# Half of a_u by seven block products, its bias prepared off VectorE, the softmax factor on ScalarE

## The chip, the cores and the metric

One Trainium2 chip, one core. The time is the device time of one execution of the whole program, in microseconds (us); the median of several executions is given. Engines are called PE (TensorE matmuls), PEld (its weight loads), DVE (VectorE), ACT (ScalarE), POOL (GpSimd) and SP (the sequencer that issues most loads).

## The reference, cut to what matters

One decoder block on 512 tokens with 1024 channels. The parts that the change touches:

```python
z = h @ w_in                        # columns: a_u | a_v | q | k | v | qi | ki | wi | g_a | g_b
y_a = gelu(a_u) * mixed             # a_u: 512 x 1024
# mixed, for chunk n of 128 tokens and group g of 128 channels:
#   sum_s tril(w_s[g])[t, s] * layer_norm(gelu(a_v))[n, s, g, c] + b_s[g, t]
p = softmax(att)                    # attention: 4 blocks of 128 queries, 8 heads, selected keys
o = p @ v
merged = sigmoid(g_a) * (y_a @ w_proj_a) + sigmoid(g_b) * (y_b @ w_proj_b)
mod = silu(c) @ w_ada + b_ada       # six sections of 1024: shift, scale, gate, twice
```

layer_norm has a gain ln_g and an offset ln_b for each channel. So mixed is the product of the masked w_s with the normalized values, times ln_g, plus a bias `ln_b * rowsum(tril(w_s)) + b_s`, and it is this bias that the kernel prepares.

## The kernel before, in words

Every fp32 product is three fp32r products: each operand is split into a high part `hi` (a copy, ACT, line 134) and a rest `lo` (a subtraction, DVE or POOL, line 138). Weights come as chunks of 128 x 1024 floats into three raw buffers; `get(i, ahead)` issues loads ahead and emits `hi` and `lo` of the chunk `ahead` places further on (`ensure`, `prep`). All engines run their instructions in the order in which the program emits them; that order is written out by hand, as lists of small tasks for each step.

The stages around the change, in order: a_v (lines 923 to 946, steps `vs` 0 to 7), which also holds the index scores; a_u (line 1051), four groups of two chunks, each chunk 24 matmuls of 512 columns; then twice `xround` (lines 1095 to 1136), which makes half of g_a by seven block products instead of eight, followed each time by two groups of the projection of y_a (`W_PA`). A round is 7 x 8 x 3 = 168 matmuls of 256 columns. Its seven weight chunks are blocks of w_in or sums of blocks, and the sums are made in DRAM by POOL's transfers (`x_moves`, line 265, eight for a round, one of them at each call of `x_move`).

`au_tasks` and `au_post` run before and after each chunk of these stages, with the step numbers of `austep`. They hold the normalization of a_v, `mix_mm` and `mix_ev` (the mixing, eight times), `rs_mm` and `bias_mix` (the row sums by a product with ones, and the bias, eight DVE instructions), and the top-k selection (`BG`: 35 pieces). The modulation's dot products (`dot`, line 209, 128 x 1024 on DVE, each behind a load of 512 KB) are put between weight chunks in the stream: eight beside a_u, four beside `W_PA`, eight beside `W_GB`, four beside `W_PB`.

The attention loop (lines 1260 to 1281) has 16 units: the query blocks i = 3, 2, 1, 0 in that order, four pairs of heads each; block i has (i + 1) x 128 keys. At step s it emits, in this order: the product with v of unit s - 3 (`at_pv`) and its split `yh` (ACT), `yl` (DVE); scores and maximum of unit s (`at_qk` on PE, `at_soft_a` on DVE); transposes of unit s - 2 (`at_T`) with the split `th` (ACT), `tl` (DVE); the softmax factor of unit s - 1 (`at_soft_b`, DVE: a reciprocal and two multiplications); the split `qh` (ACT), `ql` (DVE) of the queries of unit s + 2; the exponential of unit s (`at_exp`, ACT); and `gb_part`, a share of the product for g_b (`W_GB`), which in steps 1, 2, 6, 8, 10, 12, 14 and 16 also emits `hi` and `lo` of one weight chunk, and with it, where there is one, a dot product ahead of them. `at_pv` of unit s - 3 reads the `tl` of the step before.

Of the kernel before, what the change touches and what calls it, by code (L numbers as in the profile page):

```python
# [16 lines left out]
S = 512  # L17
# [11 lines left out]
def block_kernel(ctx: ExitStack, tc: tile.TileContext, x, x_t, c_row, positions, w_ada_t, w_first, w_in, w_blocks,  # L29
                 gmlp_w_s, gmlp_b_s, w_proj_a, w_proj_b,  # L30
                 w_out, w_ffn_in, w_ffn_out, final_norm_g, small, consts, out):
# [226 lines left out]
    W_AV = [[add_w(w_in, [k0, k0 + 1], 1024 + 512 * h, 512, V if k0 % 4 else P) for k0 in range(0, 8, 2)] for h in range(2)]  # L258
    W_AU = [group(w_in, 256 * g, pool=2, mods=mm_, mraw="acc") for g in range(4)]
    xsum = {(r, n): dram.tile([128, 1024], F32, name=f"xsum{r}{n}") for r in range(2) for n in (1, 2, 3, 4)}  # L260

# [8 lines left out]

    xm = [fn for r in range(2) for fn in x_moves(r)]

# [616 lines left out]

    def load_bs():  # L890
        late["bsb"] = mid.tile([128, 8, 128], F32, name="bsb", tag="A3", bufs=1)
        P.dma_start(late["bsb"], bass.AP(tensor=gmlp_b_s.tensor, offset=gmlp_b_s.offset,
                                         ap=[[0, 128], [128, 8], [1, 128]]))

# [4 lines left out]
    def mask_ws():  # L899
        P.affine_select(late["wmT"], late["wmT"], pattern=[[0, 8], [1, 128]], compare_op=OP.is_ge, fill=0.0, base=0,  # L900
                        channel_multiplier=-1)
        late["ones"] = mid.tile([128, 2, 128], F32, name="ones2", tag="ql", bufs=2)[:, 0]
        P.memset(late["ones"], 1.0)

    VT = {0: [load_ws, lambda: rows_a(1), lambda: rows_b(1)],
          1: [lambda: h_hi("S1"), lambda: h_hi("S4"), lambda: h_lo("S1"), lambda: h_lo("S4")],
          2: [lambda: rows_a(2), lambda: rows_b(2), lambda: h_hi("S3")],
          3: [lambda: h_lo("S3")],
          5: [mask_ws],
          7: [load_bs]}  # L910
    for _ in range(16):
# [12 lines left out]
    for h in range(2):  # L924
        pb = [bank(k, "pav") for k in range(4)]
        for i in W_AV[h]:
            for fn in VT.get(vs, []):
                fn()
            if vs % 2:
                x_move()  # L930
            if iu[1] < 24:
                idx_accs()
            else:
                run_bg(2.0)
            if vs in (5, 6):
# [46 lines left out]

    def rs_mm():
        late["rs"] = [bank(5 + k, "rs") for k in range(2)]
        for k, p in enumerate(late["rs"]):
            T.matmul(p, late["ones"], late["wmT"][:, 4 * k:4 * k + 4].rearrange("p a n -> p (a n)"), start=True, stop=True)

    def bias_mix():
        for m in range(8):
            b = late["bsb"][:, m]  # L990
            V.scalar_tensor_tensor(b, late["rs"][m // 4][:, 128 * (m % 4):128 * (m % 4) + 128], lnbc[:, m:m + 1], b,
                                   op0=OP.mult, op1=OP.add)

    ub = {}
    austep = [0, 0]
    AT = {3: [0], 4: [1, 2], 5: [3], 6: [4], 7: [5], 8: [6], 9: [7]}

    def au_post():
        s = austep[1]
        austep[1] += 1  # L1000
        if s == 2:
            rs_mm()
        for m in AT.get(s, []):
            mix_mm(m)
        while ylate and ylate[0][0] < s:
            ylate.pop(0)[1]()

    def au_tasks():
        s = austep[0]
        austep[0] += 1  # L1010
        if s == 0:
            assert iu[1] == 24
            for tk in range(4):
                ln_v(tk, 1)
            rstd(rva, mva[:, :, 1], 4, 1.0)
            V.scalar_tensor_tensor(nmr, mva[:, :, 0], -1.0, rva, op0=OP.mult, op1=OP.mult)
        elif s < 3:
            ln_v2(2 * s - 2)
            ln_v2(2 * s - 1)
        elif s == 3:  # L1020
            bias_mix()
        while ylow:
            ylow.pop(0)()
        for m in AT.get(s - 1, []):
            mix_ev(m)
        while zlate:
            zlate.pop(0)()
        for _ in range(BG.get(s, 0)):
            run_bg(0.1)
        if s < 9:  # L1030
            x_move()
        elif s == 9:
            assert not xm
        elif s == 27:
            k_b()
        if s in (28, 29):
            at_split(s - 28)

    BG = {1: 2, 2: 2, 3: 2, 4: 2, 5: 1, 6: 1, 12: 1, 13: 1, 14: 1, 15: 2, 16: 1, 17: 2, 18: 1,
          19: 1, 20: 1, 21: 1, 22: 1, 23: 1, 24: 1, 25: 1, 26: 3, 27: 2, 28: 2, 29: 2}  # L1040
    zlate = []
# [8 lines left out]

    for g in range(4):
        opt_b(W_AU[g], 8, hT, nbanks(), au_evac(g), au_tasks, au_post)

# [83 lines left out]

    def ga_evac(r):
        t = {}

        def ev(z, zb):
            c, th = z % 2, z // 2
            if c not in t:
                t[c] = mid.tile([128, 2, S], F32, name="sg", tag=f"A{c}", bufs=1)
                for m in range(2):
                    sig[4 * r + 2 * c + m] = t[c][:, m]
            A.activation(t[c][:, :, 256 * th:256 * th + 256], zb, AF.Sigmoid)
        return ev
# [850 lines left out]
    for tk in range(2):  # L1999
# [85 lines left out]
```

## Time and profile before

| | us |
|---|---|
| median of 3 runs | 792.31 |
| the runs | 791.01 to 793.17 |
| the profiled execution | 791.98 |
| its span in the profile | 790.0 |
| PE busy in the span | 778.3 |
| DVE busy | 663.7 |
| ACT busy | 443.2 |
| POOL busy | 181.4 |

A matmul's busy time overlaps that of the next one, so the distance from start to start is what one costs; where that distance stays even, PE has no gap. A row of the timeline gives start, duration, engine, line, operation, output and inputs, shape, and in brackets the idle time before it and what ended that. Rows of equal instructions in a run are merged (x2); the time of the single one is then found from the start of the next row.

### The profile page before, as it was taken

To read this page: it belongs to the slowest core of one execution; us is meant where nothing else is said; L and a number is where in the kernel's file an instruction comes from. 1 tells how busy PE (TensorE), PEld (TensorE's weight loads), DVE (VectorE), ACT (ScalarE), POOL (GpSimd) and SP (SyncE) were. 2 spreads that over 40 slices of the span, in tenths; PEclk is the share of its full clock that TensorE was granted. 3 is DMA by queue.
4 is the path that set the end of the run, shared out by engine and by line. 5 is a ranking of instruction groups with operands and counts; after the bars stand their busy time and mean duration, and the time that the engine had idled before them with its cause. 6 is when DMAs were issued, how large, how long until landed. Compare 5 with 4: busy or idle time off the path is not lost.

```text
span 790.0 us, 12600 instructions
## 1 busy us (share of the span) xinstructions
PE 778.3 (99%) x4747; PEld 694.5 (88%) x4747; DVE 663.7 (84%) x1114; ACT 443.2 (56%) x777; POOL 181.4 (23%) x220
## 2 busy tenths in 40 slices
PE   8999999999999999999999999999999999999996
PEld 6779988878988988988888899999999999878885
DVE  5988887688897799886787879889999888898777
ACT  6556455443362636666536577555665566576654
POOL 2064234574353501000010000313121322100001
PEclk9999999999999999999999999999999999999999
DMA  9959454789763733148692503989998968666664
GB/s 361 416 156 242 119 146 122 217 231 243 212 215 107 235 112 107 54 135 278 232 234 56 187 1 107 255 251 268 258 259 222 260 201 212 177 200 209 209 192 147
DMA packets 89887, 155.05 MB, mean 196 GB/s; under 512 B 7010, under 2 KB 54770, under 8 KB 89635
## 3 DMA queue, kind: packets, MB, share of 16 engines
q1 hardware_dynamic: 72976, 116.05, 44.6%
q0 software_dynamic: 15952, 37.17, 20.9%
q10 hardware_dynamic: 898, 1.04, 0.4%
q8 instruction: 37, 0.61, 0.3%
q14 instruction: 24, 0.19, 0.1%
HBM read 150.16 MB, written 33.56 MB: 233 GB/s over the span
## 4 chain that ended last, share of the span: by engine, by line
PE 64%; DVE 17%; DMA 9%; ACT 5%; issue 4%; POOL 0%; SPq 0%; POOLq 0%; ACTq 0%; DVEq 0%
PE R L66 5%; PE R L68 5%; PE R L67 5%; PE pb L66 5%; PE pb L67 5%; PE pb L68 5%; DMA mraw<-in_w_ada_t_dram 3%; DMA raw<-in_w_ffn_in_dram 3%; DMA raw<-in_w_ffn_out_dram 3%; PE pfo L67 2%; PE pfo L68 2%; PE pfo L66 2%; PE pav L66 2%; PE pav L67 2%; PE pav L68 2%
## 5 line engine op out<-in xcount | busy, mean ns | idle before, releaser
L134 ACT ACTIVATE hi<-raw 128x1024 fp32r<-128x1024 f32 (+1 forms) x111 | 114.5, 1032 | 81.6 <-PE pb L67 32.4
L138 DVE TENSOR_TENSOR lo<-raw,hi 128x1024 fp32r<-128x1024 f32 (+2 forms) x77 | 90.3, 1174 | 26.9 <-ACT hi L134 26.0
L138 POOL TENSOR_TENSOR lo<-raw,hi 128x1024 fp32r<-128x1024 f32 x27 | 69.5, 2577 | 100.2 <-ACT hi L134 69.6
L67 PE MATMUL pfo<-lo,za 128*128 128x512 f32 (+1 forms) x144 | 55.5, 386 | 0.2 <-DVE lo L138 0.2
L66 PE MATMUL pfo<-hi,za 128*128 128x512 f32 (+1 forms) x144 | 55.5, 385 | 0.0
L68 PE MATMUL pfo<-hi,za 128*128 128x512 f32 (+1 forms) x144 | 55.3, 384 | 0.0
L209 DVE CUSTOM_DVE_ANT_0 mraw<-mraw,scb,cols 128x1024 f32<-128x1024 f32 x24 | 37.6, 1568 | 11.7 <-DMA mraw<-in_w_ada_t_dram 11.7
L66 PE MATMUL R<-tb,sx 128*128 128x256 f32 x160 | 45.0, 281 | 0.3 <-ACT gr L462 0.3
L67 PE MATMUL R<-tb,sx 128*128 128x256 f32 x160 | 44.3, 277 | 0.0
L68 PE MATMUL R<-tb,sx 128*128 128x256 f32 x160 | 44.3, 277 | 0.0
L68 PE MATMUL R<-tb,lo 128*128 128x256 f32 x160 | 44.2, 277 | 0.0
L67 PE MATMUL R<-tb,hi 128*128 128x256 f32 x160 | 44.2, 276 | 0.0
L66 PE MATMUL R<-tb,hi 128*128 128x256 f32 x160 | 44.2, 276 | 0.0
L66 PE MATMUL pb<-h,hi 128*128 128x512 f32 (+1 forms) x112 | 42.7, 382 | 0.0
L68 PE MATMUL pb<-h,lo 128*128 128x512 f32 (+1 forms) x112 | 41.9, 374 | 0.0
L67 PE MATMUL pb<-h,hi 128*128 128x512 f32 (+1 forms) x112 | 41.9, 374 | 0.0
L351 POOL COPY sm<-sm 128x1 f32<-128x1 f32 x36 | 23.2, 644 | 78.7 <-ACT sm L350 78.7
L331 POOL DMA_DIRECT2D wsum<-in_w_ffn_out_dram x24 | 21.2, 885 | 78.0 <-DMA wsum<-wsum 46.1
L66 PEld LDWEIGHTS pfo<-hi,za 128*128 128x128 f32 x144 | 27.1, 188 | 6.1 <-ACT ps L1925 0.6
L67 PEld LDWEIGHTS pfo<-lo,za 128*128 128x128 f32 x144 | 27.1, 188 | 6.1 <-DVE lo L138 0.9
L68 PEld LDWEIGHTS pfo<-hi,za 128*128 128x128 f32 x144 | 27.1, 188 | 5.2
L66 PEld LDWEIGHTS R<-tb,sx 128*128 128x128 f32 x160 | 30.1, 188 | 0.9 <-ACT gr L462 0.5
(398 smaller groups left out, 2697.0 us busy)
## 6 DMA issues: line engine op xcount, KB each, us to landing
raw<-in_w_ffn_in_dram SPq DMA_DIRECT2D x44, 512.0 KB, 5.7
raw<-in_w_in_dram SPq DMA_DIRECT2D x30, 512.0 KB, 3.8
wsum<-in_w_ffn_out_dram POOLq DMA_DIRECT2D x30, 512.0 KB, 8.3
mraw<-in_w_ada_t_dram SPq DMA_DIRECT2D x24, 512.0 KB, 6.3
raw<-wsum SPq DMA_DIRECT2D x20, 512.0 KB, 3.8
s<-in_w_ada_t_dram SPq DMA_DIRECT2D x16, 512.0 KB, 8.8
raw<-in_w_ffn_out_dram SPq DMA_DIRECT2D x16, 512.0 KB, 4.6
xsum<-in_w_blocks_dram POOLq DMA_DIRECT2D x12, 512.0 KB, 6.3
```

Of the source, the lines that this page charges most:

```text
L66: T.matmul(o, wh, rh, start=start, stop=False, **kw)
L67: T.matmul(o, wh, rlo, start=False, stop=False, **kw)
L68: T.matmul(o, wlo, rh, start=False, stop=stop, **kw)
L134: A.activation(hi[:, :m], e["raw"][:, :m], AF.Copy)
L138: e["lo"].tensor_sub(lo[:, :m], e["raw"][:, :m], f(hi[:, :m]))
L209: V.tensor_tensor_reduce(out=raw[:, o], in0=raw[:, o], in1=c, scale=1.0, scalar=col if o.start else bias, op0=OP.mult, op1=OP.add, accum_o ...
L331: P.dma_start(wsum[n][o], src, accum_op=OP.add)
L351: P.tensor_copy(t, t)
```

## The change

- `W_AU` has two groups instead of four. The other half of a_u is a third `xround`, put first, so that the order is: two groups of a_u, rounds 0 and 1 back to back, two groups of `W_PA`, round 2, two groups of `W_PA`. The same stages have 33 steps instead of 30. There are 24 `x_moves` instead of 16, spread over more steps; a_v takes one at every step instead of every second.
- The row sums are no longer a product. The weights w_s come a second time in the other layout (`gmlp_w_n`), POOL masks them, ACT sums each row while copying (`row_sums`), one transpose on PE and two small transfers bring the sums to all partitions, ACT multiplies by ln_b (`rs_scale`), and a transfer with addition adds b_s (`add_bs`). `rs_mm` and `bias_mix` are gone.
- POOL clears the score tiles at the start of a_v (`clear`).
- The eight dot products beside a_u and the eight in `W_GB`'s stream become sixteen with slots of their own (`gd_load`, `gd_run`): one at the end of each attention step from 1 to 16, after `gb_part`. Sections are worked through in the same order.
- In attention the reciprocal comes directly after the maximum, and the two multiplications by it are ACT's.
- `AT` and `BG`, which say at which step mixing and top-k run, are set anew for the 33 steps.

The diff, cut (host-side inputs and signatures are left out):

```diff
-    W_AU = [group(w_in, 256 * g, pool=2, mods=mm_, mraw="acc") for g in range(4)]
+    W_AU = [group(w_in, 256 * g, pool=2) for g in range(2)]
...
-    xm = [fn for r in range(2) for fn in x_moves(r)]
+    xq = [list(x_moves(r)) for r in range(3)]
+    xm = [xq[r][n] for r, n in ((0, 0), (0, 1), (0, 2), (0, 3), (1, 0), (0, 4), (1, 1), (0, 5), (1, 2), (0, 6), (1, 3), (0, 7),
+                                (1, 4), (2, 0), (1, 5), (2, 1), (1, 6), (2, 2), (1, 7), (2, 3), (2, 4), (2, 5), (2, 6), (2, 7))]
...
-    W_GB = [group(w_in, 5192 + 256 * g, pool=2 * (g == 1), mods=mm_, nm=1, mraw=False)
+    W_GB = [group(w_in, 5192 + 256 * g, pool=2 * (g == 1))
             for g in range(4)]
     stream[W_GB[1][0]]["lo"] = V
+    gd = [next(mm_) for _ in range(16)]
+    gdt = []
+
+    def gd_load():
+        if len(gdt) < len(gd):
+            gdt.append(base.tile([128, 1024], F32, name="mraw", tag=("acc", "hs4")[len(gdt) % 2], bufs=1))
+            gd[len(gdt) - 1][0](gdt[-1])
+
+    def gd_run(k):
+        if 0 <= k < len(gd):
+            gd[k][1](gdt[k])
...
-        if h == 0:
-            P.memset(sco[i], 0.0)
...
+    def row_sums():
+        for g in range(8):
+            w = late["wn"][:, g]
+            A.activation(w, w, AF.Copy, accum_out=sm[:, g:g + 1])
+
+    def rs_out():
+        p = bank(4 + ibank[0] % 4, "rsT")
+        ibank[0] += 1
+        T.transpose(p[:8, :128], sm[:, 0:8], ident)
+        gr = tiny.tile([128, 128], F32, name="gr", tag="gr", bufs=1)
+        A.activation(gr[:8], p[:8, :128], AF.Copy)
+        A.dma_start(rsd, gr[:8])
...
+    def rs_scale():
+        for m in range(8):
+            b = late["bsb"][:, m]
+            A.activation(b, b, AF.Copy, scale=lnbc[:, m:m + 1])
+
+    def add_bs():
+        P.dma_start(late["bsb"].rearrange("p a n -> p (a n)"), rows_bcast(gmlp_b_s, D), accum_op=OP.add)
...
-            if vs % 2:
-                x_move()
+            x_move()
...
-    AT = {3: [0], 4: [1, 2], 5: [3], 6: [4], 7: [5], 8: [6], 9: [7]}
+    AT = {2: [0], 3: [1], 4: [2], 5: [3], 9: [6], 10: [7], 11: [4], 12: [5]}
...
-        if s == 2:
-            rs_mm()
...
+            rs_scale()
+            add_bs()
...
-        elif s == 3:
-            bias_mix()
...
-        if s < 9:
+        if s in (0, 1, 2, 3, 4, 6, 7, 9, 10, 12, 15, 18, 20):
             x_move()
...
-    for g in range(4):
+    for g in range(2):
         opt_b(W_AU[g], 8, hT, nbanks(), au_evac(g), au_tasks, au_post)
...
-    for r in range(2):
-        xround(r, ga_evac(r))
-        for g in (2 * r, 2 * r + 1):
+    for r in range(3):
+        xround(r, x_evac(sig, 4 * r - 4, AF.Sigmoid, "sg") if r else x_evac(ub, 4, AF.Gelu_apprx_tanh, "u"))
+        for g in (2 * r - 2, 2 * r - 1) if r else ():
             opt_b(W_PA[g], 8, yT, ((0, 1), (2, 3), (0, 1), (4, 5))[g], pa_evac(g), au_tasks, au_post)
...
-        V.reciprocal(mx[:, 6:8], mx[:, 4:6])
         for e in range(2):
-            V.tensor_scalar(pt[e][:, :n], pt[e][:, :n], mx[:, 6 + e:7 + e], None, op0=OP.mult)
+            A.activation(pt[e][:, :n], pt[e][:, :n], AF.Copy, scale=mx[:, 6 + e:7 + e])
...
     run_bg(1000)
+    gd_load()
+    gd_load()
...
             at_qk(s)
             at_soft_a(s)
+        if 1 <= s <= NU:
+            mx = AS["p", s - 1][1]
+            V.reciprocal(mx[:, 6:8], mx[:, 4:6])
...
         gb_part(GBN[s], 2 if s else 1)
+        if s:
+            gd_run(s - 1)
+            gd_load()
```

## Rows read from the trace of the kernel before

**Rows 1.** Windows by stage: from:to and length, then busy us (count) of each engine.

```profile
core 0: us, PE busy (x) PEld busy (x) DVE busy (x) ACT busy (x) POOL busy (x), PEclk, DMA share, GB/s
103.00:156.00 53.00, 52.98 (x245) 44.35 (x244) 40.55 (x57) 27.64 (x46) 25.87 (x27) 1.00 0.59 157
156.00:206.50 50.50, 50.50 (x244) 41.99 (x243) 39.86 (x80) 19.32 (x25) 28.62 (x19) 1.00 0.88 245
...
291.00:373.00 82.00, 81.89 (x484) 72.43 (x483) 68.53 (x201) 52.14 (x130) 5.59 (x5) 1.00 0.45 145
```

**Rows 2.** Timeline, PE in a_u: start, us, instruction.

```profile
155.95 0.39 PE L66 MATMUL pb<-h,hi 128*128 128x512 f32 x1
...
161.39 0.39 PE L66 MATMUL pb<-h,hi 128*128 128x512 f32 x1
...
172.27 1.88 PE L986 MATMUL rs<-wmT,ones 128*128 128x512 f32 x4
...
174.22 0.40 PE L67 MATMUL pb<-h,hi 128*128 128x512 f32 x1
```

**Rows 3.** Timeline, PE: first matmul of the second round, first one behind it.

```profile
250.28 0.28 PE L1116 MATMUL zx<-h,hi 128*128 128x256 f32 x1
...
269.54 0.40 PE L66 MATMUL pb<-y,hi 128*128 128x512 f32 x1
```

**Rows 4.** Timeline, DVE in attention steps 1 and 2.

```profile
296.64 0.16 DVE L1200 RECIPROCAL mx<-mx 128x2 f32<-128x2 f32 x1
296.83 0.88 DVE L1202 TENSOR_SCALAR pt<-pt,mx 128x512 f32<-128x512 f32 x2
...
297.97 1.28 DVE L209 CUSTOM_DVE_ANT_0 raw<-raw,scb,cols 128x1024 f32<-128x1024 f32 x1
...
299.27 1.23 DVE L138 TENSOR_TENSOR lo<-raw,hi 128x1024 fp32r<-128x1024 f32 x1
300.42 0.68 DVE L1183 CUSTOM_DVE_ANT_0 pt<-qk,sco 128x512 f32<-128x512 f32 x1
...
301.83 1.28 DVE L1274 TENSOR_TENSOR tl<-pT,th 128x512 fp32r<-128x512 f32 x2
```

**Rows 5.** Timeline, ACT in attention step 1.

```profile
296.77 0.72 ACT L1193 ACTIVATE pt<-pt,mx 128x512 f32<-128x512 f32 x1 [0.55 <-DVE mx L1185]
...
298.20 1.05 ACT L134 ACTIVATE hi<-raw 128x1024 fp32r<-128x1024 f32 x1
```

**Rows 6.** Timeline, PE: the first matmul that reads tl, in steps 3 and 4.

```profile
303.23 0.28 PE L67 MATMUL pv<-tl,v_hi 128*128 128x256 f32 x1
...
308.56 0.40 PE L67 MATMUL pv<-tl,v_hi 128*128 128x256 f32 x1
```

**Rows 7.** Single lines: ACT's copies with a factor for each partition (ns min/median/max).

```profile
L1881 ACT ACTIVATE xo<-xo,sm x1: 723/723/723, 777.7 to 777.7; 128x512 f32<-128x512 f32 x1
...
L1888 ACT ACTIVATE xo<-xo,sm x1: 615/615/615, 785.5 to 785.5; 128x384 f32<-128x384 f32 x1
```

**Rows 8.** Timeline, DVE and then ACT from attention step 8 to step 11.

```profile
335.70 1.22 DVE L138 TENSOR_TENSOR lo<-raw,hi 128x1024 fp32r<-128x1024 f32 x1
...
337.17 0.42 DVE L1183 CUSTOM_DVE_ANT_0 pt<-qk,sco 128x256 f32<-128x256 f32 x1
...
337.97 0.17 DVE L1185 TENSOR_SCALAR mx<-mx 128x2 f32<-128x2 f32 x1
...
332.49 0.42 ACT L1067 ACTIVATE qh<-qf 128x256 fp32r<-128x256 f32 x1
332.80 0.51 ACT L1193 ACTIVATE pt<-pt,mx 128x256 f32<-128x256 f32 x1
...
333.78 1.05 ACT L134 ACTIVATE hi<-raw 128x1024 fp32r<-128x1024 f32 x1
335.78 0.38 ACT L1263 ACTIVATE yb<-pv 128x256 fp32r<-128x256 f32 x1 [0.95 <-PE pv L68]
...
345.60 0.38 ACT L1263 ACTIVATE yb<-pv 128x256 fp32r<-128x256 f32 x1 [0.81 <-PE pv L68]
```

**Rows 9.** Waits of DVE in attention: us in total, times, longest.

```profile
DVE yb L1264 <- ACT yb L1263: 9.1, 8, 1.7
```

More of the change, by code (lines that the diff above doesn't have):

```diff
@@ L258, in block_kernel @@
     W_AV = [[add_w(w_in, [k0, k0 + 1], 1024 + 512 * h, 512, V if k0 % 4 else P) for k0 in range(0, 8, 2)] for h in range(2)]
-    W_AU = [group(w_in, 256 * g, pool=2, mods=mm_, mraw="acc") for g in range(4)]
-    xsum = {(r, n): dram.tile([128, 1024], F32, name=f"xsum{r}{n}") for r in range(2) for n in (1, 2, 3, 4)}
+    W_AU = [group(w_in, 256 * g, pool=2) for g in range(2)]
+    xsum = {(r, n): dram.tile([128, 1024], F32, name=f"xsum{r}{n}") for r in range(3) for n in (1, 2, 3, 4)}
     def blk(r, k):
@@ L297, in block_kernel @@
     NZ = 6
+    rsd = dram.tile([8, 128], F32, name="rsd")
     wsum = {n: dram.tile([11 * 128, 512], F32, name=f"wsum{n}") for n in (1, 2, 3, 4)}
@@ L888, in block_kernel, with load_wn, mask_wn, rs_in @@
     late = {}
-    def load_bs():
-        late["bsb"] = mid.tile([128, 8, 128], F32, name="bsb", tag="A3", bufs=1)
-        P.dma_start(late["bsb"], bass.AP(tensor=gmlp_b_s.tensor, offset=gmlp_b_s.offset,
-                                         ap=[[0, 128], [128, 8], [1, 128]]))
+    def load_wn():
+        late["wn"] = mid.tile([128, 8, 128], F32, name="wn", tag="A1", bufs=1)
+        P.dma_start(late["wn"], gmlp_w_n)
+    def mask_wn():
+        P.affine_select(late["wn"], late["wn"], pattern=[[0, 8], [-1, 128]], compare_op=OP.is_ge, fill=0.0, base=0,
+                        channel_multiplier=1)
+    def row_sums():
[9 more added lines that the diff above has]
+        A.dma_start(rsd, gr[:8])
+    def rs_in():
+        late["bsb"] = mid.tile([128, 8, 128], F32, name="bsb", tag="A3", bufs=1)
+        P.dma_start(late["bsb"].rearrange("p a n -> p (a n)"), rows_bcast(rsd, D))
+    def rs_scale():
[4 more added lines that the diff above has]
+        P.dma_start(late["bsb"].rearrange("p a n -> p (a n)"), rows_bcast(gmlp_b_s, D), accum_op=OP.add)
     def load_ws():
@@ L901, in mask_ws, with clear @@
                         channel_multiplier=-1)
[L902 to L907, printed above, removed]
+    def clear():
+        for i in (3, 2, 1):
+            P.memset(sco[i], 0.0)
+    VT = {0: [clear, load_ws, lambda: rows_a(1), lambda: rows_b(1)],
+          1: [load_wn, lambda: h_hi("S1"), lambda: h_hi("S4"), lambda: h_lo("S1"), lambda: h_lo("S4")],
+          2: [lambda: rows_a(2), lambda: rows_b(2), lambda: h_hi("S3"), mask_wn],
           3: [lambda: h_lo("S3")],
+          4: [row_sums],
           5: [mask_ws],
-          7: [load_bs]}
+          7: [rs_in]}
     for _ in range(16):
@@ L941, in block_kernel @@
                 opt_a_mm(pb[tk], tk, hi, lo, stream[i]["kts"], hT, 8)
+            if vs == 6:
+                rs_out()
             idx_mms(4 if vs > 2 else 3)
@@ L981, in mix_ev @@
         ylate.append((austep[0] - 1, hi))
[L983 to L992, printed above, removed]
     ub = {}
     austep = [0, 0]
-    AT = {3: [0], 4: [1, 2], 5: [3], 6: [4], 7: [5], 8: [6], 9: [7]}
+    AT = {2: [0], 3: [1], 4: [2], 5: [3], 9: [6], 10: [7], 11: [4], 12: [5]}
     def au_post():
@@ L1029, in au_tasks @@
             run_bg(0.1)
-        if s < 9:
+        if s in (0, 1, 2, 3, 4, 6, 7, 9, 10, 12, 15, 18, 20):
             x_move()
-        elif s == 9:
+        elif s == 30:
             assert not xm
-        elif s == 27:
             k_b()
[L1036 to L1040, printed above, removed]
+        if s in (31, 32):
+            at_split(s - 31)
+    BG = {1: 3, 2: 3, 3: 3, 6: 1, 7: 1, 8: 1, 9: 1, 14: 1, 15: 1, 16: 1, 17: 1, 18: 1, 19: 1, 20: 2, 21: 1,
+          22: 1, 23: 1, 24: 1, 25: 1, 26: 1, 27: 1, 28: 1, 29: 2, 30: 2, 31: 2}
+    assert sum(BG.values()) == 35
     zlate = []
@@ L1136, in xround, with x_evac @@
             au_post()
-    def ga_evac(r):
+    def x_evac(to, k0, fn, name):
         t = {}
@@ L1143, in ev @@
             if c not in t:
-                t[c] = mid.tile([128, 2, S], F32, name="sg", tag=f"A{c}", bufs=1)
+                t[c] = mid.tile([128, 2, S], F32, name=name, tag=f"A{c}", bufs=1)
                 for m in range(2):
-                    sig[4 * r + 2 * c + m] = t[c][:, m]
-            A.activation(t[c][:, :, 256 * th:256 * th + 256], zb, AF.Sigmoid)
-        return ev
-    for r in range(2):
-        xround(r, ga_evac(r))
-        for g in (2 * r, 2 * r + 1):
+                    to[k0 + 2 * c + m] = t[c][:, m]
+            A.activation(t[c][:, :, 256 * th:256 * th + 256], zb, fn)
+        return ev
+    for r in range(3):
+        xround(r, x_evac(sig, 4 * r - 4, AF.Sigmoid, "sg") if r else x_evac(ub, 4, AF.Gelu_apprx_tanh, "u"))
+        for g in (2 * r - 2, 2 * r - 1) if r else ():
             opt_b(W_PA[g], 8, yT, ((0, 1), (2, 3), (0, 1), (4, 5))[g], pa_evac(g), au_tasks, au_post)
@@ L2068 @@
         [w_in[512 * kh:512 * kh + 512, c + 256 * ch:c + 256 * ch + 256].reshape(4, 128, 256).transpose(1, 0, 2)
-         .reshape(128, 1024) for c in (4168, 4680) for kh, ch in ((0, 0), (0, 1), (1, 1), (1, 0))], axis=0)
+         .reshape(128, 1024) for c in (512, 4168, 4680) for kh, ch in ((0, 0), (0, 1), (1, 1), (1, 0))], axis=0)
     given["w_first"] = _np.concatenate([w_in[:, 3072:3328], w_in[:, 2048:2816]], axis=1)
@@ L2072 @@
     given["gmlp_w_s"] = _np.asarray(inputs["gmlp_w_s"])[0].transpose(2, 0, 1)
+    given["gmlp_w_n"] = _np.asarray(inputs["gmlp_w_s"])[0].transpose(1, 0, 2)
     for name in _INS:
```

5 lines of the change are left out of this document (3 added, 2 removed).

## The prediction

> **What bounds the kernel now.** I read the windows by stage first, then PE's timeline in each stage, then the timelines of DVE and ACT in attention. In the windows PE is busy to within 0.11 us in a_v, a_u and attention, at full granted clock [rows 1]. Busy time alone would prove little, since matmuls overlap; the timeline settles it. In a_u one chunk of 24 matmuls takes 161.39 - 155.95 = 5.44 us, 0.2267 each [rows 2], and a round of 168 matmuls 269.54 - 250.28 = 19.26 us, 0.1146 each [rows 3]. Between these starts nothing sticks out: PE sets the pace, and every other engine matters only where it makes PE wait. A microsecond taken from PE's work is a microsecond of the kernel; one taken from DVE is worth nothing by itself.
>
> Attention is the stage to look at twice. DVE works 68.53 us of its 82.00 and ACT 52.14 [rows 1], and the two pass work to each other several times a step. DVE's idle time there is mostly a wait for `yh`, 9.1 us in 8 waits [rows 9], which follows PE: there DVE is ahead.
>
> **The change part by part.** All sums are made on the profiled execution, 791.98 us, which lies 0.33 us below the median of the runs.
>
> *PE's work.* Two groups of a_u go: 4 x 5.44 = 21.76 us. A round comes: 19.26. Gain 2.5. The four matmuls of the row sums go: from 172.27 to the regular matmul at 174.22 is 1.95 us, of which one matmul's 0.23 belongs to the stream: gain 1.7 [rows 2]. The mixing keeps its 64 matmuls. The one added transpose has eight columns on one side; I take 0.1 us, between 0 and 0.23, the price of a whole 512-column matmul [rows 2]. Sum: -4.1 us (bounds -4.2 and -4.0, from the transpose).
>
> *What lies beside PE before attention, taken at nothing.* DVE loses eight dot products (1.30 us each by 297.97 to 299.27 [rows 4]) and the bias; it had 10 us idle in 50 of a_u [rows 1]. ACT gets eight row sums, eight scalings of 128 columns and seven chunks to split instead of four; it is busy 27.64 of 53 and 19.32 of 50.5 us [rows 1], and each of the small ones costs less than the 0.72 us of a 512-column copy with a factor [rows 7], so under 12 us together. The row sums stand ahead of the scores' evacuations in the fifth a_v step, and those ahead of PE's next score products: if ACT were late there, PE would stand for at most the eight row sums, under 6 us; I take zero because that step still leaves ACT more idle time than they need. POOL gets the mask, the earlier clearing (the same work), eight more DRAM transfers to issue, and one more subtraction of a chunk net (five of round 0 for four of a_u); behind each of its waits stand these subtractions, for which PE waits only if the two chunks of lead are used up. POOL is busy 25.87 of 53 and 28.62 of 50.5 us [rows 1]. SP loses eight loads here; they stand ahead of the weights of g_b later, where each waits for the dot product two before it and at least one full step remains. The DMA engines are the thinnest cover: share 0.88 in a_u already [rows 1]. The eight modulation loads that leave balance the eight added moves, but a_v gets four more and a round eats chunks twice as fast as a_u. If the cover is gone, rounds 0 and 1, now back to back, wait for weights; I give 0 to 3 us and take 0, because the share of 0.88 cost PE nothing.
>
> *Attention.* By the amount of work nothing is lost: DVE gives up the 32 multiplications and takes eight more dot products, and both come to some 10 us; ACT goes from 52 to about 67 of 82. The order is another matter. What changes is a chain: ACT's two multiplications of unit s - 1 wait for the reciprocal, which waits for the maximum of unit s; behind them in ACT's queue stand `qh`, the exponential of s and then `hi` of the weight chunk; DVE's `lo` waits for that `hi`; and behind `lo` now stands the dot product, which used to run ahead of it and filled exactly this wait. Behind that stand the next `yl`, maximum and `tl`, and PE's next `at_pv` waits for `tl`.
>
> Step 1, on the clock of before. The reciprocal starts at 296.64 and is done at 296.80 [rows 4]. ACT had started the exponential at 296.77 [rows 5]; now it does two 512-column multiplications first. One alone takes 0.72 [rows 7]; the exponential has the same 0.72, and by its row and the next two a successor starts after 0.63, so the pair costs 1.26. Then `qh`, 332.80 - 332.49 = 0.31 [rows 8], the exponential with its two read-outs 298.20 - 296.77 = 1.43 and `hi` 1.05 [rows 5]: done at 296.85 + 1.26 + 0.31 + 1.43 + 1.05 = 300.9. DVE meanwhile has only `ql` to do. Then `lo`, 300.42 - 299.27 = 1.15, the dot product 1.2 (its start to that of an ordinary successor), and the maximum of unit 2 starts at 303.3 instead of 300.42. It takes 301.83 - 300.42 = 1.41, the reciprocal 0.19 [rows 4], the first half of `tl` 0.68 (1.28 for both, the second starting 0.60 after the first): ready at 305.6 to 305.7. PE wants it at 303.23 [rows 6]. Wait: 2.4 us.
>
> Step 2 carries the same on. ACT's multiplications start at 305.05; with `qh`, exponential and the next `hi` it is free at 309.1, and only then comes `yh`, whose product PE finished at about 307. `yl`, maximum, reciprocal and half of `tl` follow: 309.5 + 0.34 + 1.41 + 0.1 + 0.19 + 0.68 = 312.2. PE, 2.4 us late, wants it at 308.56 + 2.4 - 0.3 (its wait of before) = 310.7: 1.5 us more. Steps 4 and 5 have no chunk; the same sum gives 0.6 for both.
>
> From step 6 on every second step has a chunk. The loop on DVE from maximum to maximum in step 8: maximum 0.80 (337.17 to 337.97), its negation and the reciprocal 0.26, then ACT: two 384-column multiplications (0.615 alone [rows 7]) 1.07, `qh` 0.31, exponential 0.98, `hi` 1.05; then `lo` and `yl` 337.17 - 335.70 = 1.47, dot product 1.21, hand-offs 0.05 [rows 8]: 7.2 us. Step 9, with no chunk: 0.80 + 0.26 + 1.84 (until `ql` is done, behind ACT's multiplications and `qh`) + 1.21 + 0.34 = 4.45. Together 11.65; PE's pair of steps takes 345.60 - 335.78 = 9.82 [rows 8]. The same sum with the widths of the other pairs gives an excess of 1.4, 1.8, 0.9, 1.0 and, for the last, of which half counts, 0.8: 5.9 us. DVE's lead, 9.1 / 8 = 1.1 us a wait [rows 9], may absorb one such excess, so 4.8 to 5.9; I take 5.4.
>
> Attention: 2.4 + 1.5 + 0.6 + 5.4 - 0.3 (the wait of before, now inside these) = +9.6 us. Bounds: 0, if the hand-offs find slack that I don't see, and 11. Nothing behind attention changes in kind, and there PE has no idle time in which to catch up.
>
> Total: 791.98 - 4.1 + 9.6 = 797.5 us.
>
> The Trainium skill speaks against this sum. "Perfetto Trace Analysis", section "Identifying the Most-Contended Engine", takes occupancy as a fair measure of VectorE and ScalarE, and "Optimizing Scalar/DVE Operations" advises moving work to ScalarE where VectorE is saturated; by that, attention would keep its length and the time would be that of the first rival. The trace of before agrees with it as far as it goes: at 68.53 of 82 us on DVE PE hardly waits.
>
> **The rivals.**
> *A, the work decides, not the order:* DVE and ACT both stay under 70 of 82 us, the hand-offs have a step to spare, and attention keeps its length. For it: occupancy, and DVE's waits of before. Against it: the price of `tl` in step 3, where PE came only about 0.7 us after it. Time 791.98 - 4.1 = 787.9. This one ends on the other side; it decides if PE's matmul after 303.23 is not held by more than 4 us in all.
> *B, only the start stalls:* steps 1 and 2 have full-width units and no lead; later the units shrink, and DVE's 1.1 us a pair, together with the steps without chunk, absorb the rest. 791.98 - 4.1 + 4.2 = 792.1: no change.
> *C, rounds 0 and 1 starve as well:* fourteen chunks in a row with moves running beside them; +3 us on the forecast: 800.5. For it: DMA share 0.88 [rows 1]. Against it: PE didn't wait in that stretch.
>
> **How the numbers follow.** Forecast 0.50, A 0.27, B 0.16, C 0.07. About 0.3%, 2.4 us, is what a measurement of this kernel can tell from no change. So faster 0.27, same 0.16, slower 0.57. The forecast's own range is 794 to 800. The range for 8 in 10 must reach down to A, since forecast and B hold only 0.66: 788.0 to 800.5.
>
> **What the profile of the changed kernel would show.** a_u and its round: two groups at 5.44 us a chunk, rounds at 19.3 us besides the mixing, no row-sum matmuls. Attention: PE waits for `tl` in step 3 and 4, over 1 us each, DVE idle before `lo` with ACT's `hi` as its releaser in steps 1, 6, 8, 10, 12, 14, and a stage of about 91 us. An attention of 82 to 83 us would make A right and my chain wrong; one of 86, B. PE waits inside the rounds with a weight chunk as releaser would speak for C.

## The result and the profile after

The changed kernel takes 799.92 us (median; 798.44 to 802.89), the kernel before 792.34 (791.01 to 793.17): ratio 1.0102, 95% interval 1.007 to 1.0134. It is slower by some 8 us. The profiled execution is the longest of them, 802.89 us with a span of 801.1.

Windows of the changed kernel by stage, columns as in [rows 1]: a_v, then attention.

```profile
core 0: us, PE busy (x) PEld busy (x) DVE busy (x) ACT busy (x) POOL busy (x), PEclk, DMA share, GB/s
103.00:156.00 53.00, 53.00 (x247) 44.47 (x246) 42.42 (x55) 30.07 (x63) 29.80 (x32) 1.00 0.70 189
...
287.40:381.20 93.80, 84.53 (x482) 71.86 (x481) 68.28 (x186) 64.57 (x163) 4.62 (x5) 1.00 0.48 160
```

PE was busy to within 0.11 us of attention's window before [rows 1]; now it is idle for 9.3 of 93.8. DVE's work is the same to 0.25 us, as the sum of multiplications against dot products had it, and neither DVE (73%) nor ACT (69%) is anywhere near full.

In this document attention is measured from the end of the last `pb` matmul ahead of it (`pb` is the tile of the projections on either side) to the start of the first one behind it: 81.43 us before (291.49 to 372.92), 93.78 after (287.47 to 381.25). So attention starts 4.0 us earlier and lasts 12.35 us longer. What lies behind it took 419.8 us of the span here, against 417.1 before; of that more below.

Timeline of PE after the change: two chunk starts in a_u, and a whole round, as [rows 2, 3].

```profile
155.98 0.39 PE L66 MATMUL pb<-h,hi 128*128 128x512 f32 x1
...
161.42 0.39 PE L66 MATMUL pb<-h,hi 128*128 128x512 f32 x1
...
246.26 0.28 PE L1147 MATMUL zx<-h,hi 128*128 128x256 f32 x1
...
265.52 0.40 PE L66 MATMUL pb<-y,hi 128*128 128x512 f32 x1
```

The chunk still takes 5.44 us and a round 19.26: half of a_u costs a round instead of four chunks, and nothing ahead of attention waits for it.

Waits in attention after the change, by engine: us in total, times, longest.

```profile
PE pv L67 <- DVE tl L1310: 8.0, 7, 2.1
PE pv L66 <- DVE yb L1296: 1.1, 2, 0.7
...
DVE lo L138 <- ACT hi L134: 13.4, 7, 2.4
DVE ql L1100 <- ACT qh L1098: 6.1, 9, 1.7
DVE yb L1296 <- ACT yb L1295: 5.3, 7, 1.0
...
ACT pt L1232 <- DVE mx L1302: 24.3, 16, 3.1
```

Read from the bottom, this is the chain: ACT stands for DVE's reciprocal, DVE for ACT's `hi` of the weight chunk, PE for DVE's `tl`. Of the 9.1 us that DVE waited for `yh` while it was ahead of PE [rows 9], 5.3 are left, and now PE waits for DVE as well.

Step 1 and its end on PE, after the change; first ACT, then DVE, then PE.

```profile
295.77 1.04 ACT L134 ACTIVATE hi<-raw 128x1024 fp32r<-128x1024 f32 x1
...
296.85 1.23 DVE L138 TENSOR_TENSOR lo<-raw,hi 128x1024 fp32r<-128x1024 f32 x1 [1.93 <-ACT hi L134]
297.99 1.28 DVE L209 CUSTOM_DVE_ANT_0 mraw<-mraw,scb,cols 128x1024 f32<-128x1024 f32 x1
...
299.19 0.69 DVE L1214 CUSTOM_DVE_ANT_0 pt<-qk,sco 128x512 f32<-128x512 f32 x1
...
299.08 0.28 PE L66 MATMUL pv<-th,v_hi 128*128 128x256 f32 x1
301.41 0.40 PE L67 MATMUL pv<-tl,v_hi 128*128 128x256 f32 x1 [2.06 <-DVE tl L1310]
```

`hi`, `lo`, dot product, maximum, `tl`, PE: link by link as forecast, where [rows 4] had the dot product ahead of `lo`.

### The profile page after: what moved, and what is told of

It is laid out like the page before. It is cut to its first block, busy times and chain, and to the rows that moved or that the text cites. A ratio compares the mean times of both kernels' runs of the same rounds, so it can differ in the third digit from the quotient of the medians.

```text
span 801.1 us, 12814 instructions
## 1 busy us (share of the span) xinstructions
PE 779.6 (97%) x4816; PEld 695.9 (87%) x4816; DVE 658.4 (82%) x1078; ACT 464.8 (58%) x841; POOL 195.1 (24%) x231
## 4 chain that ended last, share of the span: by engine, by line
PE 64%; DVE 18%; ACT 9%; DMA 6%; issue 3%; SPq 0%; POOL 0%; POOLq 0%; ACTq 0%; DVEq 0%
PE R L66 7%; PE R L67 7%; PE R L68 7%; PE pb L68 4%; PE pb L66 4%; PE pb L67 4%; PE pfo L67 4%; PE pfo L66 3%; PE pfo L68 3%; DVE lo L138 2%; PE zx L1147 2%; PE zx L1148 2%; PE zx L1150 2%; PE pav L66 2%; PE pav L67 2%
## 5 line engine op out<-in xcount | busy, mean ns | idle before, releaser
L134 ACT ACTIVATE hi<-raw 128x1024 fp32r<-128x1024 f32 (+2 forms) x114 | 117.5, 1032 | 78.0 <-PE pb L67 23.5
L138 DVE TENSOR_TENSOR lo<-raw,hi 128x1024 fp32r<-128x1024 f32 (+2 forms) x79 | 93.7, 1187 | 45.3 <-ACT hi L134 44.9
L138 POOL TENSOR_TENSOR lo<-raw,hi 128x1024 fp32r<-128x1024 f32 x28 | 71.7, 2569 | 84.8 <-ACT hi L134 84.8
L365 POOL COPY sm<-sm 128x1 f32<-128x1 f32 x36 | 27.8, 777 | 84.2 <-ACT sm L364 84.2
L209 DVE CUSTOM_DVE_ANT_0 mraw<-mraw,scb,cols 128x1024 f32<-128x1024 f32 x32 | 40.9, 1278 | 3.4 <-DMA mraw<-in_w_ada_t_dram 3.3
L66 PEld LDWEIGHTS R<-tb,sx 128*128 128x128 f32 x160 | 30.1, 188 | 0.8 <-ACT R L1859 0.5
L1232 ACT ACTIVATE pt<-pt,mx 128x512 f32<-128x512 f32 (+3 forms) x32 | 16.3, 555 | 24.3 <-DVE mx L1302 24.3
L68 PEld LDWEIGHTS R<-tb,sx 128*128 128x128 f32 x160 | 30.1, 188 | 0.0
L67 PEld LDWEIGHTS R<-tb,sx 128*128 128x128 f32 x160 | 30.0, 188 | 0.0
```

The costliest lines, as they stand in the source:

```text
L66: T.matmul(o, wh, rh, start=start, stop=False, **kw)
L67: T.matmul(o, wh, rlo, start=False, stop=False, **kw)
L68: T.matmul(o, wlo, rh, start=False, stop=stop, **kw)
L134: A.activation(hi[:, :m], e["raw"][:, :m], AF.Copy)
L138: e["lo"].tensor_sub(lo[:, :m], e["raw"][:, :m], f(hi[:, :m]))
L209: V.tensor_tensor_reduce(out=raw[:, o], in0=raw[:, o], in1=c, scale=1.0, scalar=col if o.start else bias, op0=OP.mult, op1=OP.add, accum_o ...
```

## The experiments

The theory is that of the prediction: the order of the work in the queues of ACT and DVE lengthens a chain, not the amount. Its rivals are the amount (DVE and ACT hold more than the stage can take) and the memory (the sixteen extra loads of 512 KB). The table has all runs: times and ratios are of all executions of a kernel, attention and waits of its one profiled execution. A wait of PE is the distance of two matmul starts less the usual pitch (0.11 us for 256 columns, 0.23 for 512), summed where it is over 0.15 us.

| kernel | median us | ratio to before, 95% | attention us | PE's waits there | median less attention |
|---|---|---|---|---|---|
| before | 792.34 | | 81.43 | 0.3 | 710.9 |
| after | 799.92 | 1.007 to 1.0134 | 93.78 | 11.5 | 706.1 |
| after_again | 799.74 | 1.0096 to 1.0128 | 93.75 | 11.3 | 706.0 |
| dot_first | 792.73 | 1.0003 to 1.0023 | 86.95 | 5.0 | 705.8 |
| factor_v | 791.63 | 0.9996 to 1.0019 | 86.24 | 4.2 | 705.4 |
| dot_first_factor_v | 788.15 | 0.995 to 0.9976 | 82.58 | 0.9 | 705.6 |
| short_dots | 793.32 | 1.0005 to 1.0033 | 87.22 | 5.0 | 706.1 |
| scale_late | 791.83 | 0.9987 to 1.0015 | 84.86 | 3.2 | 707.0 |
| dot_first_scale_late | 789.94 | 0.9958 to 0.9985 | 83.18 | 1.8 | 706.8 |
| lo_pool | 796.95 | 1.0046 to 1.0076 | 89.77 | 7.9 | 707.2 |
| hi_early | 789.47 | 0.9948 to 0.9975 | 83.08 | 1.3 | 706.4 |
| hi_early_factor_v | 790.16 | 0.9971 to 0.9993 | 84.73 | 3.1 | 705.4 |
| att_only | 800.49 | 1.0093 to 1.0127 | 90.28 | 8.4 | 710.2 |
| hi_early_dot_first | 790.07 | 0.9955 to 0.9982 | 84.09 | 2.2 | 706.0 |

The last column is the first finding. It is 710 to 711 for the two kernels with the old a_u and 705.4 to 707.2 for all with the new one: the a_u part brings some 4 us whatever attention does, and what differs otherwise is attention, within the 1.8 us by which the column scatters. In the profiles attention starts at 291.49 and 291.29 us with the old a_u, and at 286.97 to 288.80 with the new one.

**The same kernel again.**

> The changed kernel as it is, for a second profile and more times. In the first one the part behind attention (from the first pgb-free matmul of the second projection on) was 3.0 us longer than before: 419.9 us from 381.2 to the end against 417.1 from 372.9. If the change causes this (another phase of weight loads, say), this profile shows it again, within 0.5 us. If it is spread between executions, this profile has it at 417 to 418 us while attention stays at 93.8 us within 0.5 and begins at 287.4. Time in either case 798 to 803 us.

Attention lasted 93.75 us from 287.84, and what lies behind it 416.6 us of a span of 798.2. So the 2.7 us more behind attention in the first profile belong to that execution, not to the change.

**The dot product ahead of the chunk.**

```diff
         low()
-        gb_part(GBN[s], 2 if s else 1)
         if s:
             gd_run(s - 1)
             gd_load()
+        gb_part(GBN[s], 2 if s else 1)
```

> The two lines that run a dot product and start the next load stand ahead of the step's weight chunk instead of behind it; nothing else changes. Theory chain: DVE's wait for ACT's hi of the chunk (13.4 us in 7 waits after the change, 1.5 to 2.4 us each) takes the 1.28 us dot product in, so each chunk step ends 1.2 us earlier: the waits of PE on tl, 2.2 and 1.5 us at the start and 1.8, 1.1, 1.9, 0.8, 1.7 us later, shrink to about 1.0, 1.0, 0.6, 0, 0.7, 0, 0.5: gain 7 to 8 us, time 791 to 793. Rival work: the sixteen dot products and ACT's scalings are simply more than the stage holds, and their place is indifferent: 799 to 801. Rival memory: the sixteen extra loads of 512 KB in the stage hold up the weights: also 799 to 801, with waits that end on DMA.

792.73 us, 7.0 less than the changed kernel on the same chip (799.74), with the same work on the same engines and the same loads: both rivals fall at once. Its waits in attention:

```profile
PE pv L67 <- DVE tl L1310: 3.5, 5, 1.3
...
DVE yb L1296 <- ACT yb L1295: 6.9, 8, 2.2
DVE ql L1100 <- ACT qh L1098: 6.1, 9, 1.7
DVE lo L138 <- ACT hi L134: 5.0, 7, 1.2
```

The seven waits for `hi` are down to 5.0 us from 13.4: 1.2 us each, the dot product. PE's wait of step 3 fell by the forecast 1.2 us (2.22 to 1.02); that of step 4 stayed at 1.51, since step 2, where it arises, has no `lo` for DVE.

**The factor on DVE again, and both.**

```diff
-            A.activation(pt[e][:, :n], pt[e][:, :n], AF.Copy, scale=mx[:, 6 + e:7 + e])
+            V.tensor_scalar(pt[e][:, :n], pt[e][:, :n], mx[:, 6 + e:7 + e], None, op0=OP.mult)
```

> The softmax factor is applied by DVE again (32 multiplications, 0.42 us each at 384 columns in the trace of before), at the same place of the order; the dot products stay behind the chunk. Theory chain: ACT's exponential, and with it hi and DVE's lo, come 1.1 us earlier in each chunk step, and in the others DVE's multiplications replace a wait of 0.64 us for qh: gain about 1 us in each chunk step, 5 to 7 us in all, time 793 to 795. Rival work: DVE, 68.3 us busy in 93.8, gets 10 us more and is the loaded engine: slower, 802 to 809. Rival memory: no change, 799 to 801.

791.63 us, 8.1 less, somewhat better than expected, although DVE has more work. That contradicts the amount outright. Of PE's 4.2 us of waits, 2.4 are a single one near the end, and what DVE was late for there is a load (timeline of DVE, step 16):

```profile
371.21 1.28 DVE L209 CUSTOM_DVE_ANT_0 mraw<-mraw,scb,cols 128x1024 f32<-128x1024 f32 x1 [2.75 <-DMA mraw<-in_w_ada_t_dram]
```

So the memory has a small share, but only once the chain no longer covers it.

> Both edits at once: what is left of the change is the half of a_u in seven products, the row sums and bias off DVE, and sixteen instead of eight dot products in attention. Theory chain: the order of DVE's and ACT's work in a chunk step is that of before, so attention keeps 0 to 2 us of its 12.3 us and the time is 787.5 to 790. The two gains overlap, since both shorten the same wait: less than the sum of the two single ones. Rival work: DVE then has 78 us of work in 82: at least 4 us of waits stay, 792 or more.

788.15 us: both edits together gain 11.6 us, less than the sum of 15.1 since they shorten the same wait. This version beats the kernel before (0.9963, interval 0.995 to 0.9976) as well as the changed one. Its window of attention:

```profile
core 0: us, PE busy (x) PEld busy (x) DVE busy (x) ACT busy (x) POOL busy (x), PEclk, DMA share, GB/s
287.20:369.90 82.70, 82.42 (x483) 72.01 (x482) 76.72 (x218) 52.81 (x131) 5.45 (x5) 1.00 0.54 178
```

DVE at 76.72 of 82.70 us holds PE up less than DVE at 68.28 of 93.80 did.

**The dot products nearly without work.**

```diff
-            for o, c in ((slice(0, 512), pc[0]), (slice(512, D), pc[1])) if (sec, kt) == (0, 0) else ((slice(0, D), scb),):
+            for o, c in ((slice(0, 512), pc[0]), (slice(512, D), pc[1])) if (sec, kt) == (0, 0) else ((slice(0, 8), scb[:, 0:8]) if short else (slice(0, D), scb),):
...
+            short.append(1)
             gd[k][1](gdt[k])
+            short.clear()
```

> The changed kernel, but the sixteen dot products of attention go over 8 of their 1024 columns (the loads stay whole; the modulations of the FFN are then not the reference's). It gives the price of the dot products' time alone, at their place behind the chunk. Theory chain: each chunk step and each other step is 1.2 us shorter on DVE; the wait for hi stays, so PE's waits in chunk steps fall as in the kernel with the dot product ahead of the chunk (792.7), and the steps between win as well: 789 to 792. Rival work: sixteen times 1.2 us are 19 us of DVE, more than the 12.3 us lost, so attention is back at 81 to 82 us: 787 to 788.5. Rival memory: the loads are still there, so nothing changes: 799 to 801.

793.32 us, and PE's waits are 5.0 us, as with whole dot products in the right place. I had expected a little more. So the time of the sixteen dot products costs 6.4 us where the change put them (799.74 to 793.32), and next to nothing with each ahead of `lo` (792.73). What remains is ACT's part of the chain (waits of PE, then of DVE): DVE still stands 13.4 us for `hi`, and as much again for `yh`, which stands behind `hi` on ACT.

```profile
PE pv L67 <- DVE tl L1313: 3.9, 5, 1.3
...
DVE yb L1299 <- ACT yb L1298: 13.5, 9, 2.1
DVE lo L138 <- ACT hi L134: 13.4, 7, 2.4
```

**ACT's multiplications behind the chunk.**

```diff
-        if 1 <= s <= NU:
-            at_soft_b(s - 1)
         low = at_split(s + 2, True) if 0 < s < NU - 2 else lambda: None
...
         gb_part(GBN[s], 2 if s else 1)
+        if 1 <= s <= NU:
+            at_soft_b(s - 1)
```

> The factor stays on ACT, but its two multiplications stand behind the exponential and the weight chunk instead of ahead of them; the dot products stay behind the chunk. Amount of work on each engine: unchanged. Theory chain: the exponential and hi come 1.1 us earlier in each step, as with the factor on DVE (791.6), and the multiplications lie in ACT's idle time before yh: 791 to 794. Rival work: the same work on the same engines, no change: 799 to 801. A second rival: the multiplications now delay yh and th, for which DVE's yl and tl wait: the gain is lost again, 797 or more.

> The last edit together with the dot product ahead of the chunk: all the work of the change on the engines it chose, in another order. Theory chain: 787 to 790, as with the dot product first and the factor on DVE (788.2), since lo then finds hi ready 1.1 us earlier and the dot product lies in the wait. Rival work: 799 to 801 again; something in between would say that ACT's place behind the chunk costs the next step.

791.83 and 789.94 us. The same work on the engines that the change chose, in another order, gives back 8 to 10 us. A new wait appears, PE's transposes for the factor (1.0 us in 4, `pT <- ACT pt`), since the factor is now late.

**`lo` on POOL.**

```diff
-    W_GB = [group(w_in, 5192 + 256 * g, pool=2 * (g == 1))
+    W_GB = [group(w_in, 5192 + 256 * g, pool=2)
...
-    stream[W_GB[1][0]]["lo"] = V
```

> The changed kernel, with the subtraction lo of all eight weight chunks of attention on POOL, which has one of them already (2.40 us) and is otherwise idle there. DVE then never waits for hi of a chunk and loses seven subtractions of 1.2 us. Theory chain: the link from ACT's hi to DVE is cut altogether; of the chunk step's 7.2 us the wait of 1.5 to 2.4 us and lo's 1.15 go, the step is at 4.5 us like the others, under PE's 4.9: attention 82 to 84 us, 787.5 to 790.5. A rival: POOL and DVE slow each other down when both work (POOL's one subtraction in this stage took 3.38 us before the change and 2.40 after it): if DVE's dot product and maximum stretch by 1 us beside each subtraction, some 5 us come back and the time is 792 to 795.

796.95 us and 89.77 of attention: neither the 82 to 84 of my theory nor, in its form, the rival. The edit also does less than its expectation says: only six of the eight chunks prepared in attention are `W_GB`'s; those of steps 14 and 16 are the first of `W_PB`, and their `lo` stayed on DVE. The rows tell why the time came out so: DVE's waits, POOL and DVE in step 2, then DVE in step 14.

```profile
DVE yb L1295 <- ACT yb L1294: 7.6, 10, 1.2
...
DVE lo L138 <- ACT hi L134: 3.7, 2, 2.2
...
298.22 2.41 POOL L138 TENSOR_TENSOR lo<-raw,hi 128x1024 fp32r<-128x1024 f32 x1 [11.47 <-ACT hi L134]
...
298.70 1.95 DVE L1215 TENSOR_SCALAR mx<-mx 128x2 f32<-128x2 f32 x1
300.57 0.15 DVE L1301 RECIPROCAL mx<-mx 128x2 f32<-128x2 f32 x1
...
365.33 1.23 DVE L138 TENSOR_TENSOR lo<-raw,hi 128x1024 fp32r<-128x1024 f32 x1 [2.22 <-ACT hi L134]
```

First, cutting the link from `hi` to `lo` doesn't cut the chain: `yh` stands behind `hi` on ACT, and DVE's `yl` waits for it, 7.6 us. The theory had to be widened: what hurts is `hi` in ACT's queue, through `lo` and through `yh`. Second, DVE's negation of two numbers for each row, 0.17 us otherwise, takes 1.95 here and ends at 300.65, with POOL's subtraction (300.63); the sixteen of them took 7.8 us, against 3.1 in the changed kernel. That is about the amount of the rival, but at another place: dot products and maxima were not stretched. Third, in step 14 the old link is whole: `lo` waits 2.22 us for `hi`, the dot product behind it another 0.72 for its load, and PE then waits 1.70 and 0.80 us. Behind these two waits PE's clock fell for a while, which is 1.55 us more of what the table counts as waits; it is told below. So half of the 7.9 us comes from a step that the edit left as it was.

**`hi` early.** `get` of the step's chunk is called ahead of the factor, and DVE's `lo` is kept back to its old place.

```diff
+        elif e["lo"] is V and late_lo:
+            late_lo[-1].append(lambda: V.tensor_sub(lo[:, :m], e["raw"][:, :m], f(hi[:, :m])))
...
+        late_lo.append([])
+        if s:
+            for k in range(gbn[0], min(gbn[0] + GBN[s], 32)):
+                get(W_GB[k // 8][k % 8 // 4])
+        lows = late_lo.pop()
         if 1 <= s <= NU:
             at_soft_b(s - 1)
...
         low()
+        for fn in lows:
+            fn()
         gb_part(GBN[s], 2 if s else 1)
```

> The changed kernel, every operation on the engine that the change gave it, factor on ACT, dot products behind the chunk; only hi of the step's weight chunk is issued earlier on ACT, behind th and ahead of the two multiplications of the factor, where ACT idles for the reciprocal (24.3 us in 16 waits after the change). DVE's lo stays where it was. Theory chain: lo finds hi done, DVE's wait of 13.4 us in 7 goes to one wait or none, the chunk step falls from 7.2 to about 5.6 us and the pair to 10.1 to 10.4, against 9.8 of PE: attention 82.5 to 85.5 us, time 788.5 to 791.5. Rival: the chain of maximum, reciprocal, ACT's factor, qh and exponential is by itself longer than PE's step, with or without hi; then the two early waits (2.2 and 1.5 us) and most of the rest stay, attention over 89 us, 795 or more.

789.47 us, attention 83.08: the widened theory holds. Nothing is moved to another engine, the dot products are still behind `lo`, the factor still on ACT; `hi` alone has changed its place, into ACT's wait for the reciprocal. (The weight loads that `get` issues come earlier with it; but in attention of the changed kernel ACT never waited for a load.) ACT and then DVE around step 8 of this kernel:

```profile
329.71 0.87 ACT L1313 ACTIVATE th<-pT 128x512 fp32r<-128x512 f32 x2
330.47 1.06 ACT L136 ACTIVATE hi<-raw 128x1024 fp32r<-128x1024 f32 x1
331.42 1.12 ACT L1236 ACTIVATE pt<-pt,mx 128x384 f32<-128x384 f32 x2
...
333.22 1.22 DVE L140 TENSOR_TENSOR lo<-raw,hi 128x1024 fp32r<-128x1024 f32 x1
```

The factor starts right behind `hi`, and `lo` waits for nothing; in the whole stage its waits are 0.8 us. This version beats both kernels too (0.9948 to 0.9975).

> The same with the factor on DVE as before the change. Theory chain: with hi out of the chain and no factor on ACT, attention is at PE's own 81.5 to 83 us, and the time 787 to 789, as with the dot product first and the factor on DVE (788.2); the dot product's place then no longer matters. Rival work: DVE has 78 us of work in 82 and no wait left to lose: each step with a chunk and a dot product (0.8 + 0.3 + 0.8 + 1.0 + 0.4 + 1.2 + 1.3 + 0.4 = 6.2 us) is over PE's 4.9, and the pairs are at 11 against 9.8: attention 86 us or more, 791.5 or more.

> hi of the chunk early on ACT and the dot product ahead of lo on DVE, factor on ACT. Theory chain: with hi early, lo no longer waits, so the dot product's place is indifferent: attention as with hi early alone, 83.1 us within 0.7, time 788 to 790. If the place still matters, attention is shorter by a part of 1.2 us for each chunk step, down to PE's own 81.2 us.

790.16 and 790.07 us, attention 84.73 and 84.09: both 0.3 to 1.7 us worse than the theory had it. The two profiled executions, 791.84 and 791.46 us, are among the longest of their kernels, so these lengths of attention lean high; but by the medians too the other two edits bring nothing on top of `hi` early. In the first, PE waited 1.6 us in step 4, because DVE's two multiplications of step 2 (0.88 us [rows 4]) met POOL's one subtraction:

```profile
298.56 2.41 POOL L142 TENSOR_TENSOR lo<-raw,hi 128x1024 fp32r<-128x1024 f32 x1 [29.08 <-ACT hi L136]
...
298.69 2.96 DVE L1236 TENSOR_SCALAR pt<-pt,mx 128x512 f32<-128x512 f32 x2
```

In both, PE waited at the end, 0.9 and 0.65 us, as in the kernel with the factor on DVE, behind a dot product that had waited over 2 us for its load.

**The attention part alone, on the kernel before.** `W_GB` loses its dot products, eight of them get the two slots behind the chunk, the factor goes to ACT.

> The attention part of the change alone, on the kernel before: a_u stays with four groups, row sums on PE and bias on DVE; in attention the factor goes to ACT, the reciprocal ahead, and the eight dot products of that stage get two slots of their own and stand behind the chunk in steps 1 to 8 (eight, not sixteen, since a_u keeps its own). Theory chain: steps 1 to 8 are those of the changed kernel, with its waits of 2.2, 1.5, 0.5, 1.8 and 1.1 us; in steps 10 to 15 there is no dot product, and the waits are those of the kernel with short dot products, 0.8 and 0.5; with the 0.9 us in small gaps that makes 9.3 us less the 0.3 of before: attention 90 to 91.5 us, 800 to 802. Rival: part of the loss came from the a_u part, whose later split of k and changed background work put attention's start in another state: then less than 6 us here, under 798.

800.49 us, attention 90.28, and PE's waits are those of the changed kernel: 2.21, 1.50, 0.45, 1.83, 1.18, then 0.73 and 0.45 where no dot product is left, as with the short ones (0.82 and 0.46). So 8.85 of the 12.35 us are there without the a_u part, and where both kernels have the same work in attention the waits are the same. The other 3.5 us lie in the later pairs of steps, where this kernel lacks the eight dot products that came over from a_u.

## Why the prediction was right

It said 797.5 us, and 799.92 was measured; the sum, term by term:

| term | forecast | measured in the profiles |
|---|---|---|
| PE's work ahead of attention | -4.1 | -4.0 |
| wait in step 3 | 2.4 | 2.2 |
| wait in step 4 | 1.5 | 1.5 |
| the two behind it | 0.6 | 0.5 |
| pairs of steps 6/7 to 14/15 | 5.4 | 7.3 |
| the wait of before | -0.3 | -0.3 |
| attention | +9.6 | 11.2 in waits, +12.35 in length |

Put on the profiled execution of before, what was measured gives 791.98 - 4.0 + 12.35 = 800.3 us; the medians of the changed kernel are 799.92 and 799.74.

**PE's work** was right in sum: attention starts 4.0 us earlier, and the runs hold some 4 us in all kernels with the new a_u. **The work beside PE at nothing**: right; the eight row sums took 4.1 us of ACT and the eight scalings 2.5 us, and the one wait that the view of waits lists for PE between 100 and 290 us, 0.4 before, is 0.2 now. Rival C, rounds 0 and 1 starved, did not come.

**The chain** was right in place, order and releaser, in each of the six steps named, and once more in step 16. Its step 8 was forecast at 7.2 us; DVE's maxima of steps 8 and 9 start 7.21 us apart in the changed kernel, and those of steps 9 and 10 4.88, where the sum had 4.45:

```profile
334.26 0.41 DVE L1214 CUSTOM_DVE_ANT_0 pt<-qk,sco 128x256 f32<-128x256 f32 x1
...
341.47 0.41 DVE L1214 CUSTOM_DVE_ANT_0 pt<-qk,sco 128x256 f32<-128x256 f32 x1
...
346.01 0.42 DVE L1296 TENSOR_TENSOR yb<-pv,yb 128x256 fp32r<-128x256 f32 x1 [0.58 <-ACT yb L1295]
346.35 0.41 DVE L1214 CUSTOM_DVE_ANT_0 pt<-qk,sco 128x256 f32<-128x256 f32 x1
...
344.66 1.05 ACT L1284 ACTIVATE gb<-pgb 128x512 f32<-128x512 f32 x2
345.61 0.36 ACT L1295 ACTIVATE yb<-pv 128x256 fp32r<-128x256 f32 x1
```

**The mis-sized term** is that of the pairs, 5.4 against 7.3 us, and three things are in it. The first four pairs stood at 1.4 + 1.8 + 0.9 + 1.0 = 5.1 and took 1.81 + 1.11 + 1.87 + 0.82 = 5.6 in PE's waits; the single ones differ by up to 1.0 us, in both directions, so the agreement of the sum says little about each of them. The step without a chunk is too short in it: 4.45 us left out ACT's evacuation of a gate block, which comes with every eighth part of g_b and stands ahead of `yh`; in step 9 it takes 1.05 us, and DVE waits 0.58 for `yh` behind it. Then the last pair was counted by half, 0.8 us, as if the step behind it gave something back; it cost 0.86 + 0.80 = 1.66 us, since the whole excess lies in the chunk step (6.00 us from 366.85 to 372.85 between the maxima) and is due before the next one runs. And 0.5 us was taken off because DVE's lead might absorb one excess; no such gain shows in the waits.

**The rest**, 1.15 us by which attention is longer than its waits explain, was not in the sum. Some 0.95 lies in the product with v: the matmul that ends a wait is 0.23 us ahead of the next instead of 0.11 (301.41 to 301.64 in step 3). Another 0.1 is a transpose for the modulation, which now falls into this stage (at 333.87).

**The rivals.** A, no stall, is out: 787.9 us against 799.9. It was also the time that the prediction had put beside the Trainium skill ("Perfetto Trace Analysis", "Identifying the Most-Contended Engine"), by which occupancy tells how near VectorE and ScalarE are to their limit. The runs disagree with that reading here: PE was held up with DVE at 73% and ACT at 69%, and hardly at all with DVE at 93%. B was right in the first two waits, wrong in that the later ones would be absorbed: five pairs cost 7.3 us. A did describe kernels that could be had: with the dot product first and the factor on DVE the same products take 788.15 us, and with `hi` alone moved, all else as the change has it, 789.47.

**The range**, 788.0 to 800.5, held the median but only just, and that in part by luck: the bound of 11 us for attention gives 791.98 - 4.0 + 11 = 799.0, below the median, and the 800.5 came from rival C, whose stall did not come. The chain cost 12.35 us, so both the 9.6 and its bound were too low.

## What to carry to other kernels

Where two engines pass work to each other several times a step, sum the chain in queue order, from maximum to maximum, and compare it with the bound engine's step; busy shares said nothing of this loss. Look for an operation that depends on nothing in the step but stands in the middle of the chain (`hi` here), and issue it where its engine waits anyway; and put independent work (the dot product) ahead of a waiting instruction, not behind it. When you write the sum, list every instruction in each queue of each kind of step, the ones of every fourth step too.

## What the hardware showed besides

**DVE held by POOL.** With `lo` on POOL, DVE's negation of 128x2 numbers ended within 0.02 us of POOL's subtraction whenever they met: 300.65 against 300.63 in the rows above, and so in five more steps. With `hi` early and the factor on DVE, the two 512-column multiplications that met POOL's one subtraction (2.96 us instead of 0.88) ended 0.68 us behind POOL's 300.97. The Trainium skill, "SBUF — State Buffer", section "Who interferes with whom", has it that DVE and GpSimd share one pair of ports and that it is locked, not divided; the rows agree, and show that the price doesn't depend on the size of DVE's instruction, but on what is left of POOL's. In the kernel before it was POOL that was late: its subtraction, started 0.16 us behind a dot product of DVE (304.35 to 305.63), took 3.38 us, against 2.40 in the changed kernel.

**PE's clock after waits.** With `lo` on POOL, PE waited 1.70 us up to 369.05 and 0.80 us up to 369.97. Windows of that kernel up to then and behind, columns as in [rows 1]:

```profile
362.00:370.50 8.50, 6.40 (x33) 5.03 (x32) 5.49 (x20) 3.76 (x12) 0.53 (x1) 0.99 1.02 414
370.50:374.00 3.50, 3.50 (x11) 2.77 (x11) 1.72 (x6) 2.83 (x9) 0.00 (x0) 0.54 0.82 312
```

PE was busy for 6.40 of 8.50 us, and then the granted clock was 0.54 for 3.5 us, close to the lower of its two levels (1.2 of 2.4 GHz); seven matmuls of 512 columns took 0.20 to 0.35 us more each, 1.55 us in all. No other kernel here lost clock in attention, not even the changed one with its waits of 2.2 and 1.5 us: there the granted clock was 1.00 over the stage.
